# Mixer norm sums on ScalarE and VectorE, the up products in another order, and a row chain in stages

## The chip, the cores and the metric

The kernel runs on one core of a Trainium2 chip. The metric is the device time of one execution in microseconds (us); lower is better. Five engines work side by side, each through its own queue in order: TensorE (PE, with its weight loads as PEld), VectorE (DVE), ScalarE (ACT), GpSimd (POOL) and SyncE (SP), which here issues the DMA transfers. PE reads its operands from SBUF and writes to PSUM; DRAM is reached by DMA.

## The reference

```python
def reference(x, ...):                      # x: (1, 2048, 1024) float32
    hn = rms_norm(x, g_pre_mix)
    proj = hn @ w_in                        # 1024 x 2048, cut into four parts of 512
    u_ssm, h_conv, b_gate, c_gate = ...
    y_ssm = s5_group_mixer(u_ssm, ...)      # a state-space scan, then y * sigmoid(y @ w_glu)
    y_conv = short_conv_mixer(h_conv, b_gate, c_gate, conv_w)   # b * conv3(c * h)
    y = concatenate([rms_norm(y_ssm, g_ssm_out), rms_norm(y_conv, g_conv_out)], axis=-1)
    x = x + rms_norm(y @ w_out, g_post_mix)             # 1024 x 1024
    hn = rms_norm(x, g_pre_mlp)
    m = square(relu(hn @ w_up)) @ w_down                # 1024 x 4096, 4096 x 1024
    return x + rms_norm(m, g_post_mlp)
# rms_norm(x, g) = x * rsqrt(mean(x * x) + 1e-6) * g
```

## The kernel before

Everything is float32. A float32 product is made of three matmuls on a split of both operands: a high part (the ScalarE copy rounds it) and a low part, raw minus high (`split`, L168 to L170; `mm3`, L88 to L90). A product of 128 rows, 512 columns and a depth of 512 is so a group of 12 matmuls into one PSUM tile.

The program is one function, `block_kernel`, with nested functions. PE and POOL run in the order in which the code issues their work. ACT, DVE and SP run in an order that a scheduler sets when the kernel is built; generators that are advanced between groups of matmuls (`aside`, `between`) interleave side work with the products.

The stages, in order of time: (1) input projection, scan and convolution, up to 445 us. The conv half of the mixer's output goes to DRAM (`yc_d`), 512 tokens at a time. (2) The mixer, 445 to 724: the 2048 tokens in four blocks of 512. For a block `glu` (L818) multiplies by w_glu and makes the S5 operand `mh` of the output product, high and low, with its squares; `cprep` (L800) does the same for the conv operand `mc` from `yc_d`; `wout` (L907) makes four rows of 128 tokens. A row is a branch 1 (conv half) and a branch 0 (S5 half), each of two groups of 12 matmuls into PSUM tiles A (four buffers), which are evicted with the norm's factor rr as scale (L890 on ACT, L892 on DVE). Block 0 runs the conv half of all four rows first, since the S5 half of w_out arrives later. Once per block and branch `norms` (L854) turns the sum of squares `sqs` into rr: four one-column matmuls (L858) into the PSUM tile C, of which there is one, small DVE operations, and a power on POOL (L868). (3) `first` (L1021), in the side work of block 3, and what follows `wout` start the up products; these run to 1345 us. (4) The down products to 1955, then the last norm.

The row chain: when a row is done, `rows_out` (L895) squares it and sums it up (ACT, to a junk tile), multiplies by a gain (L898), takes a root on POOL (L122, L123), adds the residual (L900), and does the same for the pre-MLP norm (L904, L906); the row goes to DRAM as `x1_d` and `hn_d`.

Both MLP products are made by Strassen's scheme: seven products j of half-sized operands in place of eight. `LEFT` and `RIGHT` say which sums of quarters a product takes, `ORDER` in which order they run:

```python
ORDER = (1, 4, 5, 7, 3, 2, 6)
LEFT  = {1: ((0,0),1,(1,1)), 2: ((1,0),1,(1,1)), 3: ((0,0),), 4: ((1,1),), 5: ((0,0),1,(0,1)), 6: ..., 7: ...}
RIGHT = {1: ((0,0),1,(1,1)), 2: ((0,0),), 3: ((0,1),-1,(1,1)), 4: ((1,0),-1,(0,0)), 5: ((1,1),), 6: ..., 7: ...}
```

So 5 and 2 need a quarter of the hidden rows alone; 1, 3, 4, 6 and 7 a sum or difference of two. `hsum` (L940, operation L946) makes these five from `hn_d` into `hs_d`, for the first two blocks during block 2 of the mixer, for the others during the up products. `xload` fetches one operand, `xbuild` (L976) transposes it on PE (L982) into PSUM tiles C, B, B, B, one for each k, and splits each (L984 the high part on ACT, L986 the low one on DVE). `wprep` (L1010) makes a left operand from w_up: a sum (L1016), then a split. `product` (L1059) runs 12 matmuls of 512 columns (2.7 us) and combines the result with others; `hidden` sends the sums of the finished quarters to DRAM.

The SBUF buffers that the change touches are rings: `s2k` (nine tiles of 128x512, used as raw input and for squares), `r4("o")` and `r4("xx")` (rows of 128x1024, two each), `b8` (14 tiles of 128x2048), `c8` (four), `w2a` and `w2b` (eight each, left operands; w2b is made after the mixer, where s2k lay), `t2`. A tile is reused only when its last reader is done.

## Time and profile before

| | |
|---|---|
| median of three runs | 1988.48 us (1987.39 to 1989.81) |
| profiled execution | 1990.73 us |
| its span in the trace | 1988.8 us |
| mean granted TensorE clock | 0.983 |
| busy: PE | 1920.9 us (97% of the span) |
| DVE | 1402.3 us (71%) |
| ACT | 865.4 us (44%) |
| POOL | 741.4 us (37%) |
| DMA | 340.34 MB, mean 171 GB/s |

The span runs from the first to the last instruction that the profile holds; the execution's time has 1.9 us around it. The rows of the trace name a source line, an operation, an output and its inputs by the program's names, and the tile's shape. A granted clock below 1 says for which part of a stretch TensorE ran slowed. A list of waits has, for an engine, the instruction that waited, the engine and tile that released it, and the sum, the count and the longest of these waits in us. In a single row a bracket says how long the engine stood idle just before it, and who ended that.

### The profile page before, as it was taken

To read this page: it belongs to the slowest core of one execution; us is meant where nothing else is said; L and a number is where in the kernel's file an instruction comes from. 1 tells how busy PE (TensorE), PEld (TensorE's weight loads), DVE (VectorE), ACT (ScalarE), POOL (GpSimd) and SP (SyncE) were. 2 spreads that over 40 slices of the span, in tenths; PEclk is the share of its full clock that TensorE was granted. 3 is DMA by queue.
4 is the path that set the end of the run, shared out by engine and by line. 5 is a ranking of instruction groups with operands and counts; after the bars stand their busy time and mean duration, and the time that the engine had idled before them with its cause. 6 is when DMAs were issued, how large, how long until landed. Compare 5 with 4: busy or idle time off the path is not lost.

```text
span 1988.8 us, 25438 instructions
## 1 busy us (share of the span) xinstructions
PE 1920.9 (97%) x8576; PEld 1572.0 (79%) x8576; DVE 1402.3 (71%) x2007; ACT 865.4 (44%) x1479; POOL 741.4 (37%) x727
## 2 busy tenths in 40 slices
PE   8899999998899799999999999999999999999996
...
GB/s 203 133 101 75 99 123 115 70 90 160 179 157 194 189 243 218 211 204 204 170 166 238 158 143 148 148 86 312 382 168 180 187 147 180 195 107 301 236 114 111
DMA packets 202002, 340.34 MB, mean 171 GB/s; under 512 B 56336, under 2 KB 64784, under 8 KB 199568
## 3 DMA queue, kind: packets, MB, share of 16 engines
...
HBM read 230.51 MB, written 106.95 MB: 170 GB/s over the span
## 4 chain that ended last, share of the span: by engine, by line
PE 80%; POOL 6%; DMA 4%; DVE 4%; issue 3%; ACT 2%; SPq 0%; DVEq 0%; POOLq 0%; ACTq 0%
PE A L89 16%; PE A L88 16%; PE A L90 16%; PE mm L88 4%; PE mm L89 4%; PE mm L90 4%; PE B L88 4%; PE B L89 4%; PE B L90 4%; PE C L89 1%; PE C L88 1%; PE C L90 1%; DMA raw<-in_xt_dram 1%; PE B L984 1%; POOL s2k L794 1%
## 5 line engine op out<-in xcount | busy, mean ns | idle before, releaser
L1016 POOL TENSOR_TENSOR t<-b 128x512 f32<-128x512 f32 x155 | 243.8, 1595 | 358.6 <-ACT w2a L169 98.3
L1130 POOL TENSOR_TENSOR t<-t,t 128x512 f32<-128x512 f32 x80 | 116.8, 1468 | 356.1 <-DMA t<-in_w_down_dram 306.5
L88 PE MATMUL mm<-xh,wh 128*128 128x512 f32 x496 | 199.3, 402 | 7.8 <-ACT wh L169 7.3
L89 PE MATMUL mm<-xl,wh 128*128 128x512 f32 x496 | 195.6, 394 | 2.1 <-DVE xl L153 2.1
L90 PE MATMUL mm<-xh,wl 128*128 128x512 f32 x496 | 195.2, 393 | 0.2 <-POOL wl L170 0.2
L170 DVE TENSOR_TENSOR b<-w2b,b 128x512 fp32r<-128x512 f32 x112 | 92.4, 864 | 134.1 <-ACT b L169 134.1
L88 PE MATMUL A<-b,c 128*128 128x512 f32 x448 | 174.5, 390 | 1.0 <-ACT b L169 1.0
L89 PE MATMUL A<-b,c 128*128 128x512 f32 x448 | 174.6, 390 | 0.6 <-DVE b L170 0.6
L90 PE MATMUL A<-b,c 128*128 128x512 f32 x448 | 174.4, 389 | 0.0
L88 PE MATMUL A<-b,w2b 128*128 128x512 f32 x384 | 150.1, 391 | 0.0
L90 PE MATMUL A<-b,w2b 128*128 128x512 f32 x384 | 149.5, 389 | 0.0
L89 PE MATMUL A<-b,w2b 128*128 128x512 f32 x384 | 149.5, 389 | 0.0
L170 DVE TENSOR_TENSOR c<-w2a,c 128x512 fp32r<-128x512 f32 x112 | 81.2, 764 | 95.8 <-ACT c L169 95.8
L1103 DVE TENSOR_TENSOR t<-t,t 128x512 f32<-128x512 f32 x160 | 126.7, 858 | 22.9 <-ACT t L1057 22.9
L169 ACT ACTIVATE b<-w2b 128x512 fp32r<-128x512 f32 x112 | 64.7, 623 | 158.4 <-PE C L90 144.7
L89 PE MATMUL B<-b,b 128*128 128x512 f32 x336 | 130.8, 389 | 0.0
L88 PE MATMUL B<-b,b 128*128 128x512 f32 x336 | 130.7, 389 | 0.0
L90 PE MATMUL B<-b,b 128*128 128x512 f32 x336 | 130.7, 389 | 0.0
L169 ACT ACTIVATE c<-w2a 128x512 fp32r<-128x512 f32 x112 | 64.9, 624 | 135.3 <-PE A L90 134.1
L88 PEld LDWEIGHTS mm<-xh,wh 128*128 128x128 f32 x496 | 94.4, 190 | 34.0 <-ACT wh L169 7.3
L88 PE MATMUL A<-b,b 128*128 128x512 f32 x256 | 107.2, 419 | 6.2 <-DVE o L892 2.3
L89 PEld LDWEIGHTS mm<-xl,wh 128*128 128x128 f32 x496 | 94.4, 190 | 21.6 <-DVE xl L153 2.9
...
## 6 DMA issues: line engine op xcount, KB each, us to landing
...
```

Source lines behind the costliest of these rows:

```text
L88: T.matmul(ps, lh, rh, start=start, stop=False)
L89: T.matmul(ps, lh, rl, start=False, stop=False)
L90: T.matmul(ps, ll, rh, start=False, stop=stop)
L169: A.activation(dst_h, raw, AF.Copy)
L170: eng.tensor_tensor(dst_l, raw, dst_h.bitcast(F32), op=ALU.subtract)
L794: G.tensor_tensor(t, t, t, op=ALU.mult)
L984: T.transpose(pt[:, t * P:(t + 1) * P], r[:, t, k * P:(k + 1) * P], ident)
L1016: eng.tensor_tensor(src, q[0], q[1], op=pm_op[LEFT[j][1]])
L1103: V.tensor_tensor(src, q[0], q[1], op=pm_op[LEFT[j][1]])
L1130: G.tensor_tensor(r[0], r[0], r[1], op=pm_op[RIGHT[j][1]])
```

## The change

It has five parts, and no matmul is added or taken away.

- **Sums of squares.** `sumsq` squares on ACT and adds on DVE for both halves; the S5 half used POOL for both. In `norms` four small DVE operations of the conv half become one with a prepared term `epsr`; the norm of the S5 half comes after the row's second group and not the first.
- **Conv operand and w_out.** Block 0's `cprep` runs in the last step of the convolution, in c8 tiles. w_out is fetched in eight whole rows of 128x1024 into r4 tiles, not sixteen halves into s2k, and split k by k; the squares of block 0's GLU come after all four of its parts.
- **Row chain.** `rows_out` is a generator in stages, advanced by `row_step` after each group; a last stage makes the difference for product 3 or 4 from the row at hand and writes it to `hs_d`.
- **Sums for the up products.** `hsum` makes 7, 1 and 6 only, in place, on DVE.
- **Up products.** ORDER is (5, 2, 4, 3, 1, 7, 6); `product` evicts by a table; all of `wprep`'s sums run on POOL, also those of the first pass that ran on DVE.

```diff
+        V.tensor_scalar(epsr[:, 4 * blk:4 * blk + 4], tmp, EPS, None, op0=ALU.mult)
...
+    def sumsq(blk, br, i, t):
+        A.activation(t, t, AF.Square)
+        if i == 0:
+            sqs[blk, br] = t
+        else:
+            V.tensor_tensor(sqs[blk, br], sqs[blk, br], t, op=ALU.add)
+    def cprep(blk):
+        h, l = (b8(), b8()) if blk else (c8(), c8())
+        mc[blk] = (h, l)
...
+                run(cprep(0))
...
-    def sumsq(blk, br, i, t):
-        if br:
-            A.activation(t, t, AF.Square)
-        else:
-            G.tensor_tensor(t, t, t, op=ALU.mult)
-        if i == 0:
-            sqs[blk, br] = t
-        else:
-            (V if br else G).tensor_tensor(sqs[blk, br], sqs[blk, br], t, op=ALU.add)
...
+            if blk == 0:
+                sgs.append(sg)
+                next(wo_steps)
+                if m:
+                    next(wo_steps)
+            else:
+                sumsq(blk, 0, m, sg)
+            row_step()
+        for m, sg in enumerate(sgs):
             sumsq(blk, 0, m, sg)
...
     def load_wo():
         for h in (1, 0):
             for k in range(4 * h, 4 * h + 4):
                 wo[k] = b8()
-            for dh in range(2):
-                for k in range(4 * h, 4 * h + 4):
-                    t = wo[k]
-                    split2(t[:, 2 * dh, :], t[:, 2 * dh + 1, :],
-                           w_out[k * P:(k + 1) * P, dh * 512:dh * 512 + 512], G if k % 2 else V)
+            raw = {}
+            for at in range(-4 if h else -2, 4):
+                ahead = at + (4 if h else 2)
+                if ahead < 4:
+                    raw[ahead] = r4("xx" if h and ahead > 1 else "o")
+                    k = 4 * h + ahead
+                    nc.sync.dma_start(out=raw[ahead], in_=w_out[k * P:(k + 1) * P, :])
+                if at < 0:
+                    continue
+                t = wo[4 * h + at]
+                for dh in range(2):
+                    split(t[:, 2 * dh, :], t[:, 2 * dh + 1, :], raw[at][:, dh * 512:dh * 512 + 512],
...
         if br:
-            V.tensor_tensor(sr, pq, rh, op=ALU.mult)
-            V.tensor_tensor(sr, sr, rh, op=ALU.mult)
-            V.tensor_scalar(sr, sr, 1.0 / DM, EPS, op0=ALU.mult, op1=ALU.add)
+            V.scalar_tensor_tensor(sr, pq, 1.0 / DM, epsr[:, 4 * blk:4 * blk + 4], op0=ALU.mult, op1=ALU.add)
         else:
             V.tensor_scalar(sr, pq, 1.0 / DM, EPS, op0=ALU.mult, op1=ALU.add)
         G.tensor_tensor(rr, sr, nhalf[:, :4], op=ALU.pow)
-        if br:
-            V.tensor_tensor(rr, rr, rh, op=ALU.mult)
         rrs[blk, br] = rr
 
...
+    def row_step():
+        for g in list(rowq):
+            if next(g, 0) == 0:
+                rowq.remove(g)
     def branch(blk, t, br, o, aside):
...
                 w = wo[4 * br + k]
                 mm3(ps, tuple(z[:, k, t * P:(t + 1) * P] for z in m),
                     (w[:, 2 * dh, :], w[:, 2 * dh + 1, :]), k == 0, k == 3)
-            if t == 0 and dh == 0:
+            if t == 0 and dh == 1 - br:
                 norms(blk, br)
-            rr = rrs[blk, br]
-            if br:
-                A.activation(o[:, sl], ps, AF.Copy, scale=rr[:, t:t + 1])
-            else:
-                V.scalar_tensor_tensor(o[:, sl], ps, rr[:, t:t + 1], o[:, sl], op0=ALU.mult, op1=ALU.add)
+            if t or dh >= 1 - br:
+                for sl, ps in pss:
+                    rr = rrs[blk, br][:, t:t + 1]
+                    if br:
+                        A.activation(o[:, sl], ps, AF.Copy, scale=rr)
+                    else:
+                        V.scalar_tensor_tensor(o[:, sl], ps, rr, o[:, sl], op0=ALU.mult, op1=ALU.add)
+                pss = []
             next(aside, None)
+            row_step()
...
     def rows_out(blk, t, o, xx):
+        hf, b = divmod(blk, 2)
         s1 = small("s1", 4)
         A.activation(junk(), o, AF.Square, accum_out=s1[:, 0:1])
         V.tensor_tensor(o, o, gpo, op=ALU.mult)
+        yield 1
         rstd(s1[:, 1:2], s1[:, 0:1], 1, 1.0 / D, s1[:, 2:3])
         V.scalar_tensor_tensor(xx, o, s1[:, 1:2], xx, op0=ALU.mult, op1=ALU.add)
         nc.sync.dma_start(out=x1_d[4 * blk + t], in_=xx)
         s3 = small("s3", 4)
         A.activation(junk(), xx, AF.Square, accum_out=s3[:, 0:1])
         V.tensor_tensor(o, xx, gmb, op=ALU.mult)
+        yield 1
         rstd(s3[:, 1:2], s3[:, 0:1], 1, 1.0 / D, s3[:, 2:3])
         A.activation(o, o, AF.Copy, scale=s3[:, 1:2])
-        dst = hn_d[blk // 2][t].rearrange("p (k b) c -> p k b c", b=2)[:, :, blk % 2, :]
+        dst = hn_d[hf][t].rearrange("p (k b) c -> p k b c", b=2)[:, :, b, :]
         nc.sync.dma_start(out=dst, in_=o.rearrange("p (k c) -> p k c", k=2))
-
...
+        j = 3 if b else 4
+        d = s2k()
+        q = [o[:, :512], o[:, 512:]]
+        V.tensor_tensor(d, q[1 - b], q[b], op=ALU.subtract)
+        nc.sync.dma_start(out=hs_d[hf][j][:, t, :], in_=d)
+    def row_in(blk, t, name="xx"):
+        xx, tt = r4(name), 4 * blk + t
+        nc.sync.dma_start(out=xx, in_=x[tt * P:(tt + 1) * P, :])
+        return xx
+    def row_done(blk, t, o, xx):
+        g = rows_out(blk, t, o, xx)
+        next(g)
+        rowq.append(g)
+    def wout_first(aside):
+        os_ = [z.rearrange("p (a b) c -> p a (b c)", b=2)[:, i, :] for z in (b8(F32), b8(F32)) for i in range(2)]
         for t in range(4):
-            xx = row_in(t)
-            o = os_[t] if blk == 0 else r4("o")
-            if blk:
-                branch(blk, t, 1, o, aside)
+            branch(0, t, 1, os_[t], aside)
+        run(aside)
+        for t in range(4):
+            xx = row_in(0, t, "xx" if t < 2 else "o")
+            branch(0, t, 0, os_[t], aside)
+            row_done(0, t, os_[t], xx)
...
-    ORDER = (1, 4, 5, 7, 3, 2, 6)
...
+    ORDER = (5, 2, 4, 3, 1, 7, 6)
...
+    def hsum(hf, t, u):
+        for j, to in ((7, 0), (1, 1), (6, 0)):
+            (k0, b0), sign, (k1, b1) = RIGHT[j]
+            q = u[:, 2 * k0 + b0, :], u[:, 2 * k1 + b1, :]
+            V.tensor_tensor(q[to], q[0], q[1], op=pm_op[sign])
+            nc.sync.dma_start(out=hs_d[hf][j][:, t, :], in_=q[to])
 
...
     def wprep(n, j, eng=G, tmp=None):
         r = wraw[n]
         q = [r[:, 2 * i + k, :] for i, k in LEFT[j][::2]]
+        h, l = (w2a(), w2a()) if j in ORDER[:4] else (w2b(), w2b())
         src = q[0]
         if len(q) > 1:
             src = (tmp or t2)()
             eng.tensor_tensor(src, q[0], q[1], op=pm_op[LEFT[j][1]])
-        h, l = (w2a(), w2a()) if j in ORDER[:4] else (w2b(), w2b())
         split(h, l, src, V)
         W[n, j] = h, l
...
-                wprep(0, n, V, s2k)
+                wprep(0, n, G, s2k)
...
-        if j in (1, 4, 5):
+        if j in (5, 2):
             st["e", j] = e = t2()
             A.activation(e, ps, AF.Copy)
+            return
+        for c, sign, old in {4: (((1, 0), 1, ("e", 2)), ((0, 0), -1, ("e", 5))),
+                             3: (((0, 1), 1, ("e", 5)), ((1, 1), -1, ("e", 2))),
+                             1: (((0, 0), 1, (0, 0)), ((1, 1), 1, (1, 1))),
+                             7: (((0, 0), 1, (0, 0)),), 6: (((1, 1), 1, (1, 1)),)}[j]:
+            src = st[old]
+            if c not in st:
+                st[c] = t2()
+            V.tensor_tensor(st[c], ps, src, op=pm_op[sign])
+        done = {4: (1, 0), 3: (0, 1), 7: (0, 0), 6: (1, 1)}.get(j)
+        if done:
+            square(st[done])
```

At three places the order of an engine's instructions shows what moved.

POOL, from the last row of block 0 to the norms of block 1. The s_ tiles are the row chain's roots, s2k the gated S5 outputs, rr_5326 and rr_5384 before (rr_5322 and rr_5392 now) the two norm factors. Before:

```order
L122 TENSOR_SCALAR s_5216<-s_5216 128x1
L123 TENSOR_TENSOR s_5216<-s_5216,nhalf 128x1
L794 TENSOR_TENSOR s2k<-s2k 128x512 x2
L798 TENSOR_TENSOR s2k<-s2k 128x512
L794 TENSOR_TENSOR s2k<-s2k 128x512
L798 TENSOR_TENSOR s2k<-s2k 128x512
L794 TENSOR_TENSOR s2k<-s2k 128x512
L798 TENSOR_TENSOR s2k<-s2k 128x512
L868 TENSOR_TENSOR rr_5326<-sr,nhalf 128x4
L868 TENSOR_TENSOR rr_5384<-sr,nhalf 128x4
```

And now:

```order
L121 TENSOR_SCALAR s_5230<-s_5230 128x1
L122 TENSOR_TENSOR s_5230<-s_5230,nhalf 128x1
L881 TENSOR_TENSOR rr_5322<-sr,nhalf 128x4
L881 TENSOR_TENSOR rr_5392<-sr,nhalf 128x4
L121 TENSOR_SCALAR s_5400<-s_5400 128x1
```

The four squares and three adds are gone from POOL; the two powers of the norms (L868, now L881) follow straight on the roots.

ACT, in the GLU of block 0 and behind it. L828 (now L829) is the sigmoid, L832 (L833) the high part of the S5 operand b_4703 (b_4720), L792 (L716) a square, L169 (L170) the high part of a w_out tile (b_4724 to b_4727; now b_4700 to b_4703). Before:

```order
L832 ACTIVATE b_4703<-s2k,gss 128x512
L828 ACTIVATE s2k<-B 128x512
L792 ACTIVATE s2k<-s2k 128x512
L169 ACTIVATE b_4724<-s2k 128x512
L832 ACTIVATE b_4703<-s2k,gss 128x512
L169 ACTIVATE b_4725<-s2k 128x512
L828 ACTIVATE s2k<-B 128x512
L832 ACTIVATE b_4703<-s2k,gss 128x512
L169 ACTIVATE b_4726<-s2k 128x512
L828 ACTIVATE s2k<-B 128x512
L169 ACTIVATE b_4727<-s2k 128x512
L169 ACTIVATE b_4724<-s2k 128x512
```

And now:

```order
L829 ACTIVATE s2k<-B 128x512 x2
L170 ACTIVATE b_4700<-o 128x512 x2
L829 ACTIVATE s2k<-B 128x512 x2
L833 ACTIVATE b_4720<-s2k,gss 128x512 x2
L170 ACTIVATE b_4701<-o 128x512 x2
L833 ACTIVATE b_4720<-s2k,gss 128x512
L170 ACTIVATE b_4702<-xx 128x512 x2
L833 ACTIVATE b_4720<-s2k,gss 128x512
L170 ACTIVATE b_4703<-xx 128x512 x2
L716 ACTIVATE s2k<-s2k 128x512 x4
L912 ACTIVATE b_4815<-A,rr_4835 128x512
```

The work on the conv operand is gone from here, with its square; both column halves of a w_out tile now follow each other, where before the first halves of all four came first; the S5 squares stand behind all eight.

DVE, at the up start, from the end of one `xbuild` to the next. L986 (now L1026) is the low part of a transposed operand from PSUM tiles B and C, L1016 a sum of w_up quarters, L170 (L171) a low part of a left operand, L1071 and L1075 (L1117) combinations of products from PSUM tile A. Before:

```order
L986 TENSOR_TENSOR b_6787<-B,b_6786 128x512 x3
L1016 TENSOR_TENSOR t_6701<-b_6304 128x512
L1016 TENSOR_TENSOR t_6707<-b_6304 128x512
L170 TENSOR_TENSOR w2b<-b_6304,w2b 128x512
L1071 TENSOR_TENSOR t_6783<-A,t_6729 128x512
L170 TENSOR_TENSOR w2b<-t_6701,w2b 128x512
L170 TENSOR_TENSOR w2a<-t_6763,w2a 128x512
L170 TENSOR_TENSOR w2b<-t_6707,w2b 128x512
L1075 TENSOR_TENSOR t_6783<-t_6783,A 128x512
L170 TENSOR_TENSOR w2a<-b_6713,w2a 128x512
L986 TENSOR_TENSOR b_6842<-C,b_6841 128x512
```

And now:

```order
L1026 TENSOR_TENSOR b_6832<-B,b_6831 128x512 x3
L171 TENSOR_TENSOR w2b<-t_6687,w2b 128x512
L1117 TENSOR_TENSOR t_6825<-A,t_6772 128x512
L171 TENSOR_TENSOR w2b<-t_6693,w2b 128x512
L171 TENSOR_TENSOR w2a<-t_6755,w2a 128x512
L171 TENSOR_TENSOR w2b<-t_6699,w2b 128x512
L171 TENSOR_TENSOR w2a<-t_6808,w2a 128x512
L1117 TENSOR_TENSOR t_6827<-A,t_6719 128x512
L1117 TENSOR_TENSOR t_6880<-A,t_6719 128x512
L171 TENSOR_TENSOR w2a<-b_6703,w2a 128x512
L1117 TENSOR_TENSOR t_6882<-A,t_6772 128x512
L1026 TENSOR_TENSOR b_6887<-C,b_6886 128x512
```

The two sums are gone from DVE (they stand on POOL); ten operations, six splits and four combinations, stand ahead of the next low part from tile C, where there were nine, two sums, five splits and two combinations.

More of the change, by code (lines that the diff above doesn't have):

```diff
@@ L143, in block_kernel @@
     xb = {}
+    ztail = act.tile([P, 4, 2], F32, name="ztail", bufs=1)
+    G.memset(ztail, 0.0)
     rb = act.tile([P, 4, BLK], F32, name="rb", bufs=1)
@@ L708, in yprep @@
             yield
+    def sumsq(blk, br, i, t):
[8 more added lines that the diff above has]
+        raw = {}
+        for i in range(-2, 4):
+            if i < 2:
+                raw[i + 2] = s2k()
+                nc.sync.dma_start(out=raw[i + 2], in_=yc_d[i + 2][:, blk * BLK:(blk + 1) * BLK])
+                if i < 0:
+                    continue
+            if i == 0:
+                yield
+            yc = raw[i]
+            A.activation(h[:, i, :], yc, AF.Copy, scale=gcv[:, i:i + 1])
+            V.scalar_tensor_tensor(l[:, i, :], yc, gcv[:, i:i + 1], h[:, i, :].bitcast(F32),
+                                   op0=ALU.mult, op1=ALU.subtract)
+            sumsq(blk, 1, i, yc)
+            yield
     events = {}
@@ L821, in glu @@
         mh[blk] = (h, l)
+        sgs = []
         for m in range(4):
@@ L927, in wout @@
+    def wout(blk, aside):
+        for t in range(4):
+            xx, o = row_in(blk, t), r4("o")
+            branch(blk, t, 1, o, aside)
             branch(blk, t, 0, o, aside)
-            if t == 3:
-                run(aside)
-            rows_out(blk, t, o, xx)
-    ORDER = (1, 4, 5, 7, 3, 2, 6)
+            row_done(blk, t, o, xx)
+        run(aside)
+    ORDER = (5, 2, 4, 3, 1, 7, 6)
     LEFT = {1: ((0, 0), 1, (1, 1)), 2: ((1, 0), 1, (1, 1)), 3: ((0, 0),), 4: ((1, 1),), 5: ((0, 0), 1, (0, 1)),
@@ L956, in hsums @@
             if t < 4:
-                us.append(hquarters(0, t, c8(F32)))
+                us.append(quarters(0, t, c8(F32)))
             yield
             if t:
-                hsum(0, t - 1, us[t - 1], s2k, (1, 6))
+                hsum(0, t - 1, us[t - 1])
                 yield
@@ L1035, in both @@
             yield
-    wout(0, iter(()), both(wo_steps, chain(yprep(1), cprep(1))))
+    wout_first(both(wo_steps, chain(yprep(1), cprep(1))))
     glu(1)
@@ L1043, in block_kernel @@
     wout(3, first())
+    while rowq:
+        row_step()
     pm_.close()
@@ L1163, in block_kernel @@
                 t = n // 2 - 1
-                u, v = hquarters(1, t, b8(F32)), b8(F32)
-                hsum(1, t, u, iter([v[:, i, :] for i in range(4)] + [t2()]).__next__)
+                hsum(1, t, quarters(1, t, b8(F32)))
     gpl = [t2() for _ in range(2)]
```

96 lines of the change are left out of this document (17 added, 79 removed).

## The prediction

> **What bounds the kernel now.** I read the page first, then a table of stretches, then the list of PE's waits, then single rows at each wait.
>
> ```profile
> PE 1920.9 (97%) x8576; PEld 1572.0 (79%) x8576; DVE 1402.3 (71%) x2007; ACT 865.4 (44%) x1479; POOL 741.4 (37%) x727
> ```
>
> PE is the bound, and the change neither adds nor removes a matmul. So only time in which PE waits or runs slowly can be won. The stretches (us; busy and count of PE, PEld, DVE, ACT, POOL; granted clock; DMA share; GB/s) say where that is:
>
> ```profile
> 440.00:480.00 40.00, 31.95 (x113) 23.46 (x113) 26.59 (x33) 19.88 (x32) 17.95 (x13) 0.83 0.66 191
> 530.00:552.00 22.00, 17.16 (x66) 13.49 (x65) 13.54 (x16) 10.60 (x14) 13.49 (x10) 0.77 0.62 159
> 600.00:614.00 14.00, 12.30 (x44) 9.81 (x43) 8.73 (x13) 6.11 (x7) 9.07 (x8) 0.76 0.29 56
> 614.00:655.00 41.00, 38.67 (x170) 31.31 (x169) 28.05 (x32) 16.50 (x26) 14.33 (x15) 1.00 0.82 263
> 655.00:690.00 35.00, 24.25 (x94) 19.16 (x93) 23.91 (x30) 15.03 (x25) 20.05 (x18) 0.80 0.49 173
> 740.00:750.00 10.00, 5.80 (x27) 5.09 (x26) 10.00 (x16) 7.77 (x15) 0.64 (x1) 0.83 0.28 111
> 750.00:1340.00 590.00, 590.00 (x2670) 490.42 (x2669) 493.93 (x658) 333.94 (x577) 236.60 (x150) 1.00 0.49 176
> ```
>
> From 750 to 1340 (the up products) PE has no idle time, so another order of the products can win nothing there. What there is to win lies ahead of it, in the other six stretches: idle 8.05, 4.84, 1.70, 2.33, 10.75 and 4.20 us, 31.9 in all. A mean clock below 1 adds to it: read as a mix of full and half rate, 0.83 over 40 us is 13.6 us at half rate, and in the same way 10.1, 6.7, 0, 14.0 and 3.4, together 47.8. What half rate costs shows after one wait:
>
> ```profile
> 600.03 0.39 PE L88 MATMUL A<-b,b 128*128 128x512 f32 x1
> ...
> 603.21 0.39 PE L90 MATMUL A<-b,b 128*128 128x512 f32 x1
> 605.30 1.56 PE L858 MATMUL C<-ones,s2k 128*128 128x1 f32 x8 [1.70 <-POOL s2k L798]
> ...
> 607.30 0.63 PE L89 MATMUL A<-b,b 128*128 128x512 f32 x1
> 607.72 0.63 PE L90 MATMUL A<-b,b 128*128 128x512 f32 x1
> ```
>
> From 600.03 to 603.21 stand 14 matmuls more, 0.227 us apart; after the wait they begin 0.42 apart: 47% of half-rate time is lost, up to 22.5 us. So at most 54 us are there to be won, in this split (idle plus 0.47 of half rate): 14.4, 9.6, 4.8, 2.3, 17.3 and 5.8. Who ended the idle time, from 440 to 760:
>
> ```profile
> PE C L858 <- POOL s2k L798: 10.9, 3, 6.2
> PE C L984 <- DVE b L986: 4.2, 1, 4.2
> PE B L88 <- ACT s2k L828: 4.1, 1, 4.1
> ...
> PE A L88 <- ACT b L832: 1.8, 1, 1.8
> PE B L88 <- DVE wrk L770: 0.9, 1, 0.9
> ```
>
> The largest is the norm's matmul L858 at three block boundaries, waiting for POOL's sums of squares.
>
> **The boundaries.** Durations of the work that moves (min/median/max ns, first and last start):
>
> ```profile
> L828 ACT ACTIVATE s2k<-B x16: 573/577/600, 449.2 to 668.3; 128x512 f32<-128x512 f32 x16
> L832 ACT ACTIVATE b<-s2k,gss x16: 706/710/727, 454.1 to 671.8; 128x512 fp32r<-128x512 f32 x16
> L792 ACT ACTIVATE s2k<-s2k x16: 616/619/635, 451.6 to 643.8; 128x512 f32<-128x512 f32 x16
> L829 DVE TENSOR_TENSOR s2k<-s2k x16: 1026/1094/2108, 449.8 to 670.2; 128x512 f32<-128x512 f32 x16
> L833 DVE SCALAR_TENSOR_TENSOR b<-s2k,gss,b x16: 740/752/1765, 455.0 to 672.7; 128x512 fp32r<-128x512 f32 x16
> L794 POOL TENSOR_TENSOR s2k<-s2k x16: 1032/1522/2204, 455.9 to 678.6; 128x512 f32<-128x512 f32 x16
> L798 DVE TENSOR_TENSOR s2k<-s2k x12: 684/692/1785, 452.9 to 644.9; 128x512 f32<-128x512 f32 x12
> L798 POOL TENSOR_TENSOR s2k<-s2k x12: 1260/1670/1777, 462.3 to 679.7; 128x512 f32<-128x512 f32 x12
> ```
>
> Per block, four squares and three adds on POOL take 4 x 1.52 + 3 x 1.67 = 11.1 us, nearly one after the other. The same on ACT and DVE takes 4 x 0.62 and 3 x 0.69, and the last add follows the last square by 0.7. The norm of the S5 half is also issued one group of 12 matmuls (2.7 us) later. So that wait goes. What is late next is the S5 operand itself, mh: after the last GLU matmul follow L828, L829, L832 and L833, 0.58 + 1.09 + 0.71 + 0.75 = 3.1 us bare. PE needs mh's last low part after the norm of the conv half (some 0.9), two groups and eleven matmuls (35 x 0.227), 8.9 us. ACT and DVE hold a backlog there: the row chain. Per row on DVE it takes two evictions, three whole-row operations and now one difference:
>
> ```profile
> 513.46 0.74 DVE L892 SCALAR_TENSOR_TENSOR c<-A,rr,c 128x512 f32<-128x512 f32 x1
> 514.26 1.28 DVE L900 SCALAR_TENSOR_TENSOR xx<-c,s,xx 128x1024 f32<-128x1024 f32 x1
> 515.46 0.74 DVE L892 SCALAR_TENSOR_TENSOR c<-A,rr,c 128x512 f32<-128x512 f32 x1
> 516.12 1.22 DVE L904 TENSOR_TENSOR c<-xx,gm 128x1024 f32<-128x1024 f32 x1
> 518.00 1.23 DVE L898 TENSOR_TENSOR c<-c,gp 128x1024 f32<-128x1024 f32 x1 [0.67 <-ACT junk L897]
> ```
>
> That is 1.48 + 1.28 + 1.22 + 1.23 = 5.2 now and 5.9 with the difference (0.69, as L798's add on DVE), where PE spends 24 x 0.227 = 5.4 us on a row of block 0. DVE falls behind by some 2 us over the four rows, and the last row's operations stand among the GLU's. I reckon 8 us of the 8.9 used, so waits of a fraction of a us remain. They are bounded by 0 and by 1.8, which PE waited for mh before (L832 in the list). I take 1.0 for each of the three boundaries, its share of half rate included. Gains: 9.6 - 1.0, 4.8 - 1.0 and 17.3 - 1.0.
>
> The last one, 655 to 690, also holds the wait of the GLU's fourth product for L828 (4.1). There the row chain was queued behind hsum, whose 12 DVE and 8 POOL operations wait for s2k buffers. Afterwards 12 remain, in place, on DVE; none needs a buffer; and they are spread over blocks 1 and 2. Eight differences of blocks 0 and 1 move into the row chain, eight more come with blocks 2 and 3 instead of the up loop, all on DVE, where blocks 1 to 3 have room: a row there is 48 matmuls, 10.9 us, against 5.9. The 2.3 of 614 to 655 goes with it.
>
> **The first block.** Of the 8.05 us idle from 440 to 480, 0.9 lie ahead of the GLU (DVE wrk L770 in the list), the other 7.1 between its end and the norm's matmul, where PE waits part by part for w_out's splits. By the new order of ACT, the last GLU sigmoid comes first, then three operations like L832 and five high parts of w_out until the last that the first group needs: 0.58 + 3 x 0.71 + 5 x 0.62 (as L792, the same shape) = 5.8 us; POOL's low part adds 1.7 (as its adds, L798), two matmuls 0.45. That is 8.0 us where 2.7 are work: 5.3 idle, plus 6.7 us of half rate as after the wait at 605, 3.2. The conv operand's preparation moves ahead into the last conv step, where it is covered, but a low part that waits for its transfer now stands ahead of the last conv product on DVE; the GLU waits for that product already (0.9) and will for 0.7 more. Loss then 5.3 + 3.2 + 1.6 = 10.1 of the 14.4: gain 4.3.
>
> The Trainium skill, "TensorE: Matmul & The Clock Gate", section on HAM oscillation, counts idle gaps above about 3.4 us as those that bring half rate. The trace disagrees on the threshold: 1.70 us at 605 was followed by 6.7 us at half rate, while 2.33 us in pieces from 614 to 655 left the clock at 1.00. By the rule the 3.2 would not be paid.
>
> **The up start.** PE's transposes for the second operand share one PSUM tile, C, and the fourth set waits for DVE's eviction of the third:
>
> ```profile
> 733.43 7.20 POOL L1016 TENSOR_TENSOR t<-b 128x512 f32<-128x512 f32 x5 [1.26 <-ACT o L906]
> 736.28 3.20 DVE L1016 TENSOR_TENSOR t<-b 128x512 f32<-128x512 f32 x2
> 739.40 1.78 DVE L170 TENSOR_TENSOR w2b<-b,w2b 128x512 fp32r<-128x512 f32 x1
> ...
> 741.71 0.67 DVE L170 TENSOR_TENSOR w2b<-t,w2b 128x512 fp32r<-128x512 f32 x1
> 745.44 1.00 PE L984 MATMUL C<-ident,b 128*128 128x128 f32 x4 [4.20 <-DVE b L986]
> ```
>
> Two sums leave DVE (3.2 us) and three join POOL, which then runs eight in a row (about 12 us). In the new order DVE has six splits and four adds ahead of the fourth eviction, and the fifth set waits, 4.3 us later. Without collision that is 10 x 0.68 = 6.8 us, and a wait of 2; with each split at 1.78 while POOL runs, 6.6 more. Ends: 2.0 + 1.6 and 8.6 + 3.2. The row at 739.40 is this very place, so I lean to the upper end: 8 us against 5.8, a loss of 2.2. The first transposes also follow straight on a norm whose tile C DVE must read first: 0.4.
>
> The Trainium skill, "SBUF — State Buffer", section "Who interferes with whom", says that a VectorE instruction with two SBUF inputs and a GpSimd instruction that reads SBUF block each other; 1.78 against 0.67 agrees. By it alone all six splits are blocked, and the loss is 6.
>
> **The up loop.** Each pass keeps eight DVE reads of PSUM, seven splits and five sums of the hidden part; ACT copies one tile less. I cost it at nothing: four A tiles of PSUM cover 8 us, and DVE is busy 494 of 590. What happens if that cover fails is the slower rival.
>
> **Sum.** 4.3 + 8.6 + 3.8 + 2.3 + 16.3 - 2.2 - 0.4 = 32.7 us. The profiled execution took 1990.73 us, 2.25 above the median of the three runs shown, 1988.48; so 1988.5 - 32.7 = 1955.8, and I write 1956.
>
> **Rivals.**
> - Short waits leave the clock alone (for it: 614 to 655; against: 605). The first block's 3.2, half of the three boundaries and the up start's half rate go: about 1948.
> - The sums only change their queue: ACT and DVE are in order, and the norm waits for the row chain as it did for POOL. Against: the norm comes 2.7 us later. For: mh was 1.8 late before. Half of the boundaries' 31.7 stays, 15: 1971.
> - Slower: three products in succession (4, 3, 1) now take two DVE operations each. With splits at 1.78, 6 x 0.69 + 4 x 1.78 = 11.3 us against 3 x 2.7 of PE; if PSUM's four tiles don't cover the 3.1, each of 32 passes loses up to 3.1, 99 us; from 1.05 a pass it eats the gain. At 2 a pass: 2019. Against it: the first two products leave DVE only the hidden sums, and DVE's 494 us of 590 already hold the collisions with POOL's present sums.
> - Nothing is won: the waits refill elsewhere (w2b now lies where the last differences' s2k tiles were): 1988.
>
> **How the numbers follow.** Chances: forecast 0.55 (its own range 1949 to 1963), full clock 0.15, same queue 0.20, slower 0.06, nothing 0.04. The range 1942 to 1975 takes in the first three; below, all but the first block's 10 and the up start's 4 is won. 0.2% (4 us) is about what a measurement here can tell from no change. Faster 0.90, same 0.04, slower 0.06.
>
> **What would show it.** In the new profile no L858-like wait on a sum; the first block still idle for 5 to 6 us behind w_out's low parts; PE's wait for C at the up start as long as before or longer, with splits of 1.6 us beside POOL; no PE wait from 750 to 1340. A wait for mh of more than 2 us, or any PE wait that recurs in the up loop, makes the prediction wrong.

## The result and the profile after

The changed kernel takes 1966.53 us (median of four runs, 1966.01 to 1971.44) against 1988.64 for the kernel before: a ratio of 0.9894 on record, 95% interval 0.9877 to 0.9912 (the medians alone give 0.9889). One execution of a kernel below, the one before with the new order, took 2222.68 us at a clock of 0.81; it is left out. The forecast was 1956, with 1942 to 1975 as its range and 1949 to 1963 as the likeliest case's own; it was 22 us faster, not 33. So the time lies inside the range, but not where the likeliest case had it. The profiled executions, which the working went by, took 1990.73 and 1966.70: 24.0 us. So 1.9 of the missing 10.6 are these executions (that of before was 2.1 us slower than its median, that of now 0.2), and the other 8.7 are in the terms; by the spans in the traces, 24.2 us apart, they are 8.5.

The engines' busy times in the profile of the changed kernel:

```profile
PE 1910.2 (97%) x8576; PEld 1564.5 (80%) x8576; DVE 1393.1 (71%) x2014; ACT 861.3 (44%) x1463; POOL 688.7 (35%) x696
```

To see where the time went, both traces are cut at the same pieces of work, not at the same times: the first matmul of each GLU (G0 to G3), the first transposes of the second and of the seventh operand of the up products (T2, T7). Stretches of before, G0-G1, G1-G2, G2-G3, G3-T2 and T2-T7 (us; busy and count of PE, PEld, DVE, ACT, POOL; granted clock; DMA share; GB/s):

```profile
446.10:518.00 71.90, 63.93 (x257) 49.97 (x258) 44.75 (x51) 39.84 (x63) 29.55 (x25) 0.91 0.49 150
518.00:583.50 65.50, 60.66 (x258) 49.49 (x257) 43.93 (x48) 35.19 (x52) 27.97 (x30) 0.92 0.60 189
583.50:647.90 64.40, 60.37 (x258) 49.02 (x256) 44.34 (x49) 28.79 (x43) 31.46 (x27) 0.95 0.62 187
647.90:706.10 58.20, 47.45 (x202) 38.29 (x201) 37.20 (x46) 23.35 (x38) 26.23 (x25) 0.88 0.53 187
706.10:751.70 45.60, 41.38 (x214) 34.68 (x213) 33.90 (x43) 28.43 (x49) 13.44 (x15) 0.96 0.63 220
```

And of the changed kernel:

```profile
448.40:513.60 65.20, 61.53 (x256) 49.95 (x257) 46.02 (x52) 38.77 (x64) 22.36 (x19) 0.92 0.56 186
513.60:571.80 58.20, 57.25 (x257) 46.60 (x256) 43.20 (x52) 34.11 (x52) 17.94 (x20) 1.00 0.62 195
571.80:634.90 63.10, 59.15 (x258) 47.66 (x257) 48.66 (x59) 35.33 (x53) 15.54 (x19) 0.97 0.75 242
634.90:681.80 46.90, 43.89 (x202) 35.90 (x201) 30.89 (x40) 24.71 (x41) 13.47 (x16) 0.96 0.53 184
681.80:726.80 45.00, 41.28 (x214) 34.11 (x212) 31.05 (x42) 26.90 (x48) 17.18 (x19) 0.96 0.79 285
726.80:1006.50 279.70, 279.70 (x1240) 231.50 (x1241) 233.51 (x313) 151.19 (x253) 108.58 (x73) 1.00 0.51 184
```

A stretch from one GLU to the next holds 240 matmuls of 512 columns and two norms: 240 x 0.227 + 2 x 0.95 = 56.4 us of PE alone; the fastest such stretch of any kernel below took 56.3, and that is used here as PE's own time. The third row of each is the one to look at: 64.4 before, 63.1 now. That block got almost nothing, and its DMA share rose from 0.62 to 0.75.

| stretch | before | now | gained | forecast |
|---|---|---|---|---|
| up to G1 (first block, with what leads to it) | 518.0 | 513.6 | 4.3 | 4.3 |
| G1-G2 (boundary of blocks 0 and 1) | 65.5 | 58.2 | 7.3 | 8.6 |
| G2-G3 (blocks 1 and 2) | 64.4 | 63.1 | 1.4 | 3.8 + 2.3 |
| G3-T2 (blocks 2 and 3, first transposes) | 58.2 | 46.9 | 11.3 | 16.3 - 0.4 |
| T2-T7 (up start) | 45.6 | 45.0 | 0.6 | -2.2 |
| T7 to the end | 1237.1 | 1237.8 | -0.7 | 0 |
| sum | | | 24.2 | 32.7 |

What PE waits for between 440 and 760 in the changed kernel (us in total, times, longest):

```profile
PE C L1024 <- DVE sr L880: 2.9, 1, 2.9
PE B L1024 <- DVE b L1026: 2.4, 1, 2.4
PE A L88 <- DVE o L914: 1.9, 2, 1.2
PE B L88 <- ACT s2k L829: 1.8, 1, 1.8
PE A L88 <- ACT b L170: 1.7, 1, 1.7
PE B L88 <- DVE wrk L802: 1.4, 1, 1.4
PE A L89 <- POOL b L171: 1.3, 1, 1.3
PE C L1024 <- DVE b L1026: 1.3, 1, 1.3
...
```

No row names a sum of squares any more (L858 <- L798 was 10.9 us). In its place stand small waits, the eight largest shown, for several operations of ACT and DVE and one of POOL.

### The profile page after: what moved, and what is told of

It reads as the page before. It is cut to its first block, busy times and chain, and to the rows that moved or that the text cites. A ratio compares the mean times of both kernels' runs of the same rounds, so it can differ in the third digit from the quotient of the medians.

```text
span 1964.6 us, 25344 instructions
## 1 busy us (share of the span) xinstructions
PE 1910.2 (97%) x8576; PEld 1564.5 (80%) x8576; DVE 1393.1 (71%) x2014; ACT 861.3 (44%) x1463; POOL 688.7 (35%) x696
## 4 chain that ended last, share of the span: by engine, by line
PE 83%; DVE 6%; DMA 3%; ACT 3%; POOL 2%; issue 2%; SPq 0%; DVEq 0%; POOLq 0%; ACTq 0%
PE A L88 16%; PE A L89 16%; PE A L90 16%; PE mm L88 5%; PE mm L90 5%; PE mm L89 5%; PE B L88 4%; PE B L90 4%; PE B L89 4%; PE C L89 1%; PE C L90 1%; PE C L88 1%; DMA raw<-in_xt_dram 1%; PE S L524 1%; PE B L1024 1%
## 5 line engine op out<-in xcount | busy, mean ns | idle before, releaser
L1055 POOL TENSOR_TENSOR t<-b 128x512 f32<-128x512 f32 x158 | 236.2, 1512 | 364.6 <-DVE t L1129 158.4
L88 PE MATMUL A<-b,c 128*128 128x512 f32 x480 | 188.4, 392 | 4.1 <-DVE t L1117 2.3
L89 PE MATMUL A<-b,c 128*128 128x512 f32 x480 | 188.6, 393 | 1.9 <-POOL b L171 1.3
L1117 DVE TENSOR_TENSOR t<-A,t 128x512 f32<-128x512 f32 x256 | 167.3, 684 | 30.1 <-PE A L90 27.2
L90 PE MATMUL A<-b,c 128*128 128x512 f32 x480 | 188.2, 392 | 0.0
L171 DVE TENSOR_TENSOR b<-w2b,b 128x512 fp32r<-128x512 f32 x112 | 93.6, 876 | 132.8 <-ACT b L170 132.8
L171 DVE TENSOR_TENSOR c<-w2a,c 128x512 fp32r<-128x512 f32 x112 | 80.5, 757 | 95.3 <-ACT c L170 95.3
L170 ACT ACTIVATE b<-w2b 128x512 fp32r<-128x512 f32 x112 | 64.6, 623 | 160.8 <-PE C L90 146.3
L1129 DVE TENSOR_TENSOR t<-t,t 128x512 f32<-128x512 f32 x160 | 104.1, 700 | 41.8 <-ACT t L1097 39.0
L170 ACT ACTIVATE c<-w2a 128x512 fp32r<-128x512 f32 x112 | 64.8, 623 | 136.6 <-PE A L90 135.5
L1096 ACT ACTIVATE t<-t 128x512 f32<-128x512 f32 x128 | 81.0, 633 | 79.6 <-DVE t L1117 79.3
```

What stands on the lines that cost most here:

```text
L88: T.matmul(ps, lh, rh, start=start, stop=False)
L89: T.matmul(ps, lh, rl, start=False, stop=False)
L90: T.matmul(ps, ll, rh, start=False, stop=stop)
L170: A.activation(dst_h, raw, AF.Copy)
L171: eng.tensor_tensor(dst_l, raw, dst_h.bitcast(F32), op=ALU.subtract)
L1055: eng.tensor_tensor(src, q[0], q[1], op=pm_op[LEFT[j][1]])
```

## The experiments

Twelve kernels were run, each beside the kernel before on the same chip. Ratios are to that; 1988.6 times the ratio stands behind it, since chips differ by a few us. The stretches are from one profile each. Where an edit leaves a stretch alone they still differ, G1-G2 from 57.9 to 58.4 in four kernels; T7 to the end took 1237.1 to 1239.4 in all. Rows whose intervals overlap are not told apart by their totals.

| kernel | ratio (95%) | us | G1-G2 | G2-G3 | G3-T2 | T2-T7 |
|---|---|---|---|---|---|---|
| before | 1 | 1988.6 | 65.5 | 64.4 | 58.2 | 45.6 |
| changed | 0.9894 (0.9877 to 0.9912) | 1967.5 | 58.2 | 63.1 | 46.9 | 45.0 |
| before, sums moved | 0.9937 (0.9920 to 0.9954) | 1976.1 | 63.0 | 60.3 | 54.6 | 45.5 |
| changed, sums back on POOL | 0.9984 (0.9973 to 0.9996) | 1985.4 | 63.3 | 69.3 | 54.8 | 44.4 |
| before, new order | 1.0011 (1.0000 to 1.0021) | 1990.8 | 65.5 | 63.3 | 59.4 | 45.2 |
| changed, row sums on POOL | 0.9919 (0.9900 to 0.9937) | 1972.5 | 64.6 | 62.6 | 49.9 | 45.1 |
| changed, no difference | 0.9866 (0.9844 to 0.9888) | 1962.0 | 58.0 | 63.7 | 43.1 | 43.0 |
| changed, no hsum operations | 0.9873 (0.9850 to 0.9896) | 1963.3 | 58.8 | 63.5 | 45.8 | 45.0 |
| changed, S5 norm in tile B | 0.9895 (0.9869 to 0.9921) | 1967.7 | 58.1 | 63.3 | 44.5 | 48.6 |
| changed, operand sums on DVE | 0.9880 (0.9860 to 0.9901) | 1964.7 | 58.4 | 63.2 | 45.9 | 45.3 |
| changed, hsum held to block 2 | 0.9897 (0.9876 to 0.9919) | 1968.1 | 57.9 | 65.5 | 45.3 | 45.0 |
| changed, difference early | 0.9860 (0.9842 to 0.9879) | 1960.8 | 56.3 | 60.7 | 47.4 | 43.4 |
| difference early, operand sums on DVE | 0.9840 (0.9824 to 0.9855) | 1956.8 | 56.3 | 60.5 | 44.5 | 44.6 |
| the same, hsum held to block 3 | 0.9892 (0.9873 to 0.9911) | 1967.1 | 56.3 | 56.9 | 61.5 | 42.7 |

### Which part made the gain

The sums alone, in the kernel before:

```diff
 def sumsq(blk, br, i, t):
-    if br: A.activation(t, t, AF.Square)
-    else:  G.tensor_tensor(t, t, t, op=ALU.mult)
+    A.activation(t, t, AF.Square)
 ...
-        (V if br else G).tensor_tensor(sqs[blk, br], ...)
+        V.tensor_tensor(sqs[blk, br], ...)
```

> The kernel before with one part of the change: the S5 half's squares on ACT and its adds on DVE, the norm where it was (after the first group). Theory 'the sum was late': PE's three waits of L858 for POOL's L798 (2.97, 1.70 and 6.22 us, with 24 us at half rate behind them) shrink to about 1 us each, because in the changed kernel the last add ends about 1 us after the place where this norm stands: 1968 to 1974 us. Rival 'the place of the norm did it': the sum is as late behind the row chain on ACT and DVE as it was on POOL, and the waits only change their releaser: 1983 to 1989.

It took 1977.87 us: 12.5 won by the ratio, where the first theory had some 15 to 21 and the rival at most 6: between the two. PE's waits in it:

```profile
PE B L88 <- ACT s2k L825: 4.8, 1, 4.8
PE C L855 <- DVE s2k L795: 4.1, 2, 2.1
```

The norm (L855 there) waits twice, 1.96 and 2.11 us, where it waited 2.97 and 6.22; the third wait is gone. Both are below the 2.7 us by which the full change issues this norm later, so the later place can cover what is left. The GLU's wait of 4.1 for its sigmoid, which isn't the sums' doing, stays (4.8).

The whole change with the sums back on POOL (the reverse edit in the changed kernel):

> The changed kernel with the S5 half's squares and adds back on POOL, the norm still after the second group. 'The sum was late': the waits come back less the 2.7 us by which the norm stands later, 0.3 and 0 at the first two boundaries and about 3 at the third, with DVE slower beside POOL: 1970 to 1977. 'The place of the norm did it': no wait for POOL at the norm, 1965 to 1968. If the sums were all of the gain: 1985 or more.

It took 1986.59, outside 1970 to 1977 and outside the rival's range: what was expected if the sums were all of the gain. They are not, since alone they won 12.5; but without them the rest of the change is worth only 3 us of some 22. The norm doesn't wait in it. What does are the matmuls that need the S5 operand's high parts. The list of PE's waits, then L833 (the GLU's multiplication, L829 before) in this kernel, and the same line (L830) in the changed one (min/median/max ns):

```profile
PE A L88 <- ACT b L836: 12.4, 5, 4.3
```

```profile
L833 DVE TENSOR_TENSOR s2k<-s2k x16: 1037/1084/2111, 451.7 to 668.4; 128x512 f32<-128x512 f32 x16
```

```profile
L830 DVE TENSOR_TENSOR s2k<-s2k x16: 1061/1088/1121, 452.4 to 652.5; 128x512 f32<-128x512 f32 x16
```

Beside POOL's sums an operation of 1.09 us takes up to 2.11, and in POOL's order the row chain's roots stand behind squares and adds (one right behind a square from 525.05 us, the next behind an add to 530.55), so the rows, the GLU behind them on ACT and DVE, and with it the operand come late. The sums cost more than the wait that showed: they slowed what feeds the next wait.

The order of the up products alone, in the kernel before (ORDER, and the table in `product`):

> The kernel before with the new order of the up products and the table of evictions alone (hsum still makes five sums, at the places it had). My working gives the order itself nothing from 750 to 1340, and at the up start only what the moved sums cost: 1986 to 1991, the wait for tile C at the up start within 2 us of 4.2. Rival 'part of the gain comes from the order' (products 5 and 2 need no sum, so the first operands are ready sooner and the row chain is clear of them): 1984 or less, and the GLU's 4.1 us wait for L828 at the last boundary smaller.

1992.4, a ratio of 1.0011 whose interval begins at 1.0000: nothing won. PE's wait for C at the up start was 2.9, for 4.2 before, as expected within 2; the GLU's wait for its sigmoid 5.2, not smaller than 4.1. If the order is worth something in the changed kernel, it is through what it lets the row chain do; no run here shows that.

### What is late now: the row chain's sums

Both row sums moved to POOL (`V` to `G` at L940 and L990 of the changed kernel):

> The changed kernel with the row chain's difference (L940) and hsum's three operations (L990) on POOL and not on DVE. Theory 'DVE's queue': in the changed trace DVE stands 1.62 us at 577.5 because the difference waits for ACT's scaling of the row, and five hsum operations stand ahead of the last row's evictions; the GLU's wait for its sigmoid (1.80, then 3.4 us at half rate) goes, 4 to 6 us over the boundaries: 1960 to 1964. Rival 'POOL's queue takes over': POOL in program order holds the next root behind a difference that waits for ACT, and DVE slows beside it: 1967 to 1975.

1974.25, the rival's range, but its reasons are seen only in part. At G1-G2 6.4 us are lost. The longest of PE's waits there, 2.59 us up to 548.89, is for a row's evictions. These wait for the norm's power on POOL, and that for DVE's read of C (L880), which stands behind low parts; the difference on POOL is not seen in that chain. PE's waits, and the power:

```profile
PE A L88 <- DVE o L914: 5.7, 2, 3.1
```

```profile
546.60 1.46 POOL L881 TENSOR_TENSOR rr<-sr,nhalf 128x4 f32<-128x4 f32 x1 [7.72 <-DVE sr L880]
```

The 3.1 comes in block 2, up to 621.02. There the rival's slow DVE is seen: ahead of the eviction two of its whole-row operations, L926 and L930, took 2.30 and 2.32 beside hsum's sums on POOL, where the same operations took 1.28 and 1.22 in the kernel before (L900, L904).

Left out, one at a time (these two kernels then compute other numbers). The difference:

```diff
-    d = s2k()
     q = [o[:, :512], o[:, 512:]]
-    V.tensor_tensor(d, q[1 - b], q[b], op=ALU.subtract)
-    nc.sync.dma_start(out=hs_d[hf][j][:, t, :], in_=d)
+    nc.sync.dma_start(out=hs_d[hf][j][:, t, :], in_=q[b])
```

> The changed kernel without the subtraction of the row chain: a quarter of the row goes to hs_d as it is (left out: sixteen DVE subtractions, so products 3 and 4 get other numbers). Theory 'the difference holds DVE': it waits for ACT's scaling of the row (1.62 us at 577.5) with the last row's evictions behind it, and takes 0.69 us of each row; without it the stretch from GLU 2 to GLU 3, 63.1 us where PE's own work is 56.3, falls to 59 to 60, and the two other boundaries by 0.5 to 1: 1960 to 1963 against 1966.5. Rival 'something else in the queue' (hsum, or ACT's order): that stretch stays above 62, 1965 to 1967.

1963.38; the total is near the first theory's range, but not from its place. G2-G3 stayed at 63.7; the gain, 5.8 us, came behind G3.

hsum's twelve operations for the first half:

> The changed kernel without hsum's twelve DVE operations for the first two blocks (left out, so products 7, 1 and 6 of the first half get raw quarters; their transfers stay). Theory 'hsum holds DVE': six of them stand ahead of row 3's evictions at 566 to 579, so the GLU's fourth part gets its sigmoid in time (now 1.80 late, then 3.4 us at half rate): GLU 2 to GLU 3 falls from 63.1 to 59 or 60, 1962 to 1964. Rival 'the row chain alone is late': 62 or more, 1965 to 1967. If both this kernel and the one without the difference gain 3, either load is enough to make DVE late there.

1964.72, and G2-G3 again 63.5. Neither load on DVE alone sets that stretch: each time the GLU's wait of 1.80 us for its sigmoid is gone, but other waits have come behind it, 3.0 for the S5 operand's high parts without the difference, 3.4 for a row's eviction without hsum's operations. In the second trace two rows of ACT point at transfers (start, duration, operation, in brackets the idle time before it and who ended it):

```profile
559.73 0.72 ACT L735 ACTIVATE b<-s2k,cw 128x512 fp32r<-128x512 f32 x1 [3.92 <-DMA s2k<-yc_d]
...
597.52 1.22 ACT L711 ACTIVATE w2a<-s2k 128x512 fp32r<-128x512 f32 x1 [2.66 <-DMA s2k<-y_d]
```

Inputs of a later block arrive late, and ACT, in order, holds the row's work behind them. That led to the runs on transfers. Only the second row lies between G2 and G3, though; the first wait comes back, 2.73 us at 559.89, with hsum held back, so it isn't hsum's.

### hsum's transfers

hsum's quarters (1 MB each, and three writes of 256 KB) held back to block 2 by a one-column copy ahead of the load:

```diff
 def quarters(hf, t, u):
+    if hf == 0:
+        V.tensor_copy(u[:, 0, 0:1], rrs[2, 1][:, 0:1])
     nc.sync.dma_start(out=u, in_=hn_d[hf][t])
```

> The changed kernel with hsum's quarters for the first two blocks held back: a one-column DVE copy from block 2's conv norm into each quarter's tile ahead of its load, so the loads (four of 1 MB) and the twelve writes can't start before block 2. Theory 'hsum's transfers': in place, hsum needs no s2k buffer and is hoisted to the end of block 1, where DMA is full (580 to 600: share 1.04, before 0.53), and the next block's inputs (ACT waits 3.9 for yc_d in the kernel without hsum's sums) come late; held back, GLU 2 to GLU 3 falls from 63.1 to 58 or 59, and at most 2 come back at the last boundary: 1961 to 1964. Rival 'the row chain's length on ACT and DVE': GLU 2 to GLU 3 stays at 62 or more, because hsum now stands among block 2's own rows: 1965 to 1970.

1968.46: the rival's range. The stretch G2-G3 cut at 606, in the changed kernel:

```profile
571.80:606.00 34.20, 31.43 (x137) 25.02 (x135) 26.71 (x33) 20.04 (x30) 7.46 (x9) 0.95 0.93 288
606.00:634.90 28.90, 27.71 (x123) 22.64 (x122) 21.95 (x26) 15.28 (x24) 8.09 (x11) 1.00 0.54 189
```

And with hsum held back:

```profile
571.70:606.00 34.30, 33.69 (x154) 27.13 (x154) 25.01 (x33) 20.41 (x31) 8.16 (x10) 1.00 0.66 207
606.00:637.20 31.20, 25.66 (x105) 20.74 (x104) 24.18 (x33) 15.64 (x24) 7.59 (x11) 0.89 0.92 308
```

In the first part DMA falls from 0.93 to 0.66 and PE's idle time from 2.8 to 0.6; in the second DMA rises from 0.54 to 0.92, and PE's idle time from 1.2 to 5.5. There PE and ACT wait:

```profile
PE A L88 <- ACT o L912: 5.5, 1, 5.5
```

```profile
ACT b L735 <- DMA s2k<-yc_d: 4.4, 2, 2.5
```

The loss went where hsum went. Its transfers and its operations moved together here, and the copy itself held DVE for 2.20 us at 611.52, waiting for a buffer that a write still used.

Held back once more, behind block 3's inputs, in the version of the next part (`sqs[3, 1]` in place of `rrs[2, 1]`, and `hsums()` after `cprep(3)`):

> The same, and hsum's quarters held back until the last conv operand's squares are summed, so that hsum's 4 MB of loads and 3 MB of writes stand behind the loads of block 3's inputs and not in front of any. Theory 'the wait follows hsum's transfers': held back to block 2 they moved the loss from the boundary (63.1 to 57.9 from GLU 1 of that pair on, waits 0.28 and 0.28) into block 2 (ACT's wait for yc_d, PE 5.54); with nothing left to be late, GLU 2 to GLU 3 falls to 57 or 58 in this one, 2 to 3 us: 1955 to 1958. Rival 'hsum's twelve operations then meet the last boundary', where before had the GLU waiting 4.1 for its sigmoid: 1960 or more.

G2-G3 fell to 56.9, PE's own 56.3 all but reached. The whole took 1970.51, the rival's case: the transfers and the operations meet the last boundary, and the first transposes wait.

```profile
PE C L1026 <- DVE s2k L1057: 8.5, 1, 8.5
```

The operand that these transposes read is fetched from 659.50 us on, 9.3 us later than in the changed kernel. So of the 6.8 us that this stretch takes beyond 56.3 in the changed kernel, hsum's place decides 3.6 (60.5 to 56.9), after the early difference of the next part had won 2.6 (63.1 to 60.5). Its twelve operations alone don't explain that (63.5 without them); that its transfers do is argued and not shown, since no run moved them without the operations. A place for its 7 MB that costs nothing was not found.

### The last boundary and a better version

Two ways of taking away the wait of the first transposes for C. The S5 norm's columns in a tile B:

> The changed kernel with the S5 norm's four columns in a tile B of PSUM (three buffers) and not in C (one). Theory 'tile C': the 2.90 us wait of the first transposes for DVE's read of C (L880), with 3.4 us at half rate behind it, goes: GLU 3 to the second transposes falls from 46.9 to about 42.5, 1962 us. Rival 'the read itself is late': L880 still stands behind four low parts that wait for ACT and POOL, so the row's evictions are late, and PE waits for a tile A instead: 45 or more, 1965 to 1967. A B tile held so long can also hold the GLU or the transposes: up to 1970.

1967.94. The wait for C was gone, G3-T2 fell by 2.4, and T2-T7 rose by 3.6: PE came earlier to transposes whose rows weren't there (2.8 us for DMA b<-hn_d). Neither theory had that.

The first four left operands' sums on DVE (`wprep(0, n, V, s2k)` in `first`):

> The changed kernel with the sums of the first four left operands (those in the side work of block 3) back on DVE; the later three stay on POOL. Theory 'the queue behind POOL': at 656 to 662 DVE's low parts wait for ACT's high parts, these for POOL's sums (2.65 us), and the norm's read of C stands behind them; with the sums on DVE the wait of 2.90 falls to 1 to 1.5, and GLU 3 to the second transposes from 46.9 to 44 or 45: 1963 to 1965. Rival 'DVE is the queue anyway': two sums of 0.69 join the same queue, 46.5 or more: 1966 to 1969.

1965.54, between the two; the wait fell from 2.90 to 0.26, more than expected, and G3-T2 by 1.0 only, since PE now waited 1.14 for the S5 operand.

The difference taken ahead of ACT's scaling, and scaled on ACT:

```diff
     V.tensor_tensor(o, xx, gmb, op=ALU.mult)
     ...
+    V.tensor_tensor(d, q[1 - b], q[b], op=ALU.subtract)
     yield 1
     rstd(s3[:, 1:2], ...)
     A.activation(o, o, AF.Copy, scale=s3[:, 1:2])
+    A.activation(d, d, AF.Copy, scale=s3[:, 1:2])
     ...
-    yield 1
-    V.tensor_tensor(d, q[1 - b], q[b], op=ALU.subtract)
     nc.sync.dma_start(out=hs_d[hf][j][:, t, :], in_=d)
```

> The changed kernel with the difference taken ahead of ACT's scaling of the row and scaled by ACT itself (0.62 us more on ACT for each row), so that DVE doesn't wait for L933 (0.6 to 2.1 us for each row now). Theory 'the wait in DVE's queue': the evictions behind it come earlier, and what the kernel without the difference gained behind GLU 3 (5.8 us: 2.5 up to the first transposes, 1.3 and 2.0 behind them) comes for the most part, 3 to 5: 1961 to 1964. Rival 'the operation and its transfer, not the wait': DVE's 0.69 stays, ACT gets 0.62: 1965 to 1970.

1961.70, the size that the first theory had, but from another place: 4.3 at G1-G2 and G2-G3 and 1.6 at the up start, none at the first transposes. G1-G2 is at 56.3, PE's own time. DVE does the same work. In the changed kernel the difference waited for ACT, here between 560 and 582, and this wait is gone:

```profile
DVE s2k L940 <- ACT o L933: 2.6, 2, 1.6
```

The edit also takes one stage out of the row chain and puts 0.7 us for each row on ACT, and its interval still touches the changed kernel's.

Both together:

> A version to beat the changed kernel: the difference ahead of ACT's scaling (as in the run before, 1961.7) and the first four left operands' sums on DVE. Theory 'two separate waits': the C wait of 3.79 us falls below 1 as it did with the sums on DVE alone (2.90 to 0.26), about 3 us: 1958 to 1960. Rival 'the wait moves on': what PE gains there it loses again at the S5 operand (1.14 and 0.37 with the sums on DVE alone) or at the up start, which waits for the last rows' transfers: 1961 to 1963.

1959.76, ratio 0.9840 (0.9824 to 0.9855), below the changed kernel's interval: the fastest version, by the ratios 10.7 us below the changed kernel (the kernel before took 1993.0 on that chip). The total is the first theory's; its wait for C was 2.0, not below 1.

## Why the prediction was right and wrong

By stretches the three boundaries fell short of the forecast by 1.3, 4.7 and 4.6 us and the end by 0.7, while the up start came out 2.8 better: that the total is only 8.5 off is in part luck, since errors cancel.

**The sums of squares: right in kind.** The waits of L858 are gone and the norm's later place covers the rest. The prediction put the sums' price at the wait alone; with them back on POOL the change is worth 3 us, since they also slow DVE and hold the roots. The Trainium skill, "SBUF — State Buffer", section "Who interferes with whom", has a VectorE instruction of two SBUF inputs and a GpSimd one that reads SBUF block each other; 1.09 against 2.11 for the GLU's multiplication agrees.

**"I take 1.0 for each of the three boundaries": the step that failed.** Left over are 58.2 - 56.3 = 1.9 at the first, 6.8 at the second, and at the third 4.6 more than the forecast's sum. The reckoning compared DVE's work for a row with PE's, 5.9 against 10.9 us, and found room in blocks 1 to 3. But the row chain is a chain: each step waits for another engine, and what stands behind it in the queue waits too. At the second boundary, DVE of the changed kernel:

```profile
574.51 1.41 DVE L990 TENSOR_TENSOR c<-c 128x512 f32<-128x512 f32 x2
577.54 0.69 DVE L940 TENSOR_TENSOR s2k<-o 128x512 f32<-128x512 f32 x1 [1.62 <-ACT o L933]
578.15 0.74 DVE L914 SCALAR_TENSOR_TENSOR o<-A,rr,o 128x512 f32<-128x512 f32 x1
578.81 0.68 DVE L990 TENSOR_TENSOR c<-c 128x512 f32<-128x512 f32 x1
579.41 0.75 DVE L914 SCALAR_TENSOR_TENSOR o<-A,rr,o 128x512 f32<-128x512 f32 x1
```

PE's last matmul of that row began at 571.59; its evictions L914 stand behind a difference that waits for ACT and behind hsum. ACT's queue then passes it on: the row's square waits for the eviction, and the GLU's first sigmoid (L829) for the square.

```profile
580.25 1.06 ACT L922 ACTIVATE junk<-o 128x1024 bf16<-128x1024 f32 x1 [2.74 <-DVE o L914]
581.31 0.58 ACT L829 ACTIVATE s2k<-B 128x512 f32<-128x512 f32 x1
```

That is the rival "the sums only change their queue", with the row chain and not the sums in front. It had half of 31.7 us staying, 1971; the result lies between it and the forecast, 4.5 us from the one and 10.5 from the other.

**"None needs a buffer; and they are spread over blocks 1 and 2": what it left out.** Work that waits for nothing can also come too early. Before, hsum's writes began at 613.7 us, and two of its four loads of 1 MB stood ahead of block 3's first inputs (y_d, fetched from 595.5 on). In place its writes begin at 568.2, and three loads and six writes stand ahead of these inputs (593.1), the fourth load close behind. That the missing buffers had kept hsum late is the likeliest reading; no run gave them back. The 3.8 + 2.3 of that stretch became 1.4; with the difference early and hsum held back it came within 0.6 us of PE's own time.

**The first transposes, "0.4".** They wait 2.90 us for DVE's read of C (L880). It stands behind low parts that wait for ACT's high parts, which wait for POOL's sums of w_up:

```profile
658.39 1.93 DVE L171 TENSOR_TENSOR w2a<-s2k,w2a 128x512 fp32r<-128x512 f32 x2 [1.84 <-ACT w2a L170]
660.72 1.29 DVE L171 TENSOR_TENSOR w2a<-b,w2a 128x512 fp32r<-128x512 f32 x2 [0.40 <-ACT w2a L170]
661.93 0.15 DVE L880 TENSOR_SCALAR sr<-C 128x4 f32<-128x4 f32 x1
```

The prediction looked for the effect of the sums' move to POOL at the up start only. With them on DVE the wait was 0.26.

**The first block: right in the sum, by luck.** Two terms are off and cancel. Idle time was 1.75 + 1.30 + 0.6 = 3.6 for 5.3. Half rate was forecast as 6.7 us; the clock of 0.92 over G0-G1's 65.2 us reads as 10.4, which costs 4.9 for 3.2. The wait for the last conv product was 1.4 for 1.6. And G0 itself came 2.4 us later than before, of which that wait explains 0.5. In this and in every other profile that keeps the change's early part, PE waits 1.3 to 3.2 us for DVE near 95 us, where the kernels built on before wait at most 0.4; no run took that apart, and it stays open.

**The up start: better than forecast.** The six splits ahead of the fourth eviction weren't slowed, since POOL's eight sums were over before they began; they cost the lower bound. What met POOL's sums was the last row's difference, 1.80 for 0.69 after a wait of 0.69 for ACT, and PE waited 2.4 for a tile B whose low part stands behind it. POOL's sums, then two rows of DVE:

```profile
707.84 6.67 POOL L1055 TENSOR_TENSOR t<-b 128x512 f32<-128x512 f32 x5
715.67 3.76 POOL L1055 TENSOR_TENSOR t<-b 128x512 f32<-128x512 f32 x3 [1.17 <-issue]
```

```profile
709.08 1.80 DVE L940 TENSOR_TENSOR s2k<-o 128x512 f32<-128x512 f32 x1 [0.69 <-ACT o L933]
...
720.04 0.68 DVE L171 TENSOR_TENSOR w2b<-t,w2b 128x512 fp32r<-128x512 f32 x1
```

**The up loop** went as forecast: 279.70 of 279.70 us busy from T7 to the second half's first transposes (its row is the last of the changed kernel's stretches), and no wait that recurs; the one wait there, 2.3 us, stands at the end of the up products (1339.45).

**The clock.** The rival of full clock after short waits fell in this kernel: the GLU's 1.80 us wait was again followed by half rate, matmuls beginning 0.43 us apart in place of 0.23:

```profile
581.94 0.50 PE L88 MATMUL B<-w2a,c 128*128 128x512 f32 x1 [1.80 <-ACT s2k L829]
...
584.16 0.63 PE L89 MATMUL B<-w2a,c 128*128 128x512 f32 x1
584.59 0.63 PE L90 MATMUL B<-w2a,c 128*128 128x512 f32 x1
```

The Trainium skill, "TensorE: Matmul & The Clock Gate", section on HAM oscillation, has gaps above about 3.4 us bring half rate; no wait of this kernel between G0 and T7 was that long (the longest was 2.9), and half rate came in four places there, so here too the trace disagrees. Length alone doesn't decide either: in the fastest version a wait of 2.04 us for C left the clock at 1.00.
